# Dilated attention's last head pair: its small transfers on ScalarE's DMA queue, one token tile held back for it, four head-pair outputs split ahead of the last tile of values

## The chip, the cores and the metric

The kernel runs on one core of one Trainium2 chip. A time is the device time of one execution in microseconds (us). Before the change it is 2256.52 us, the median of three runs from 2256.39 to 2257.5.

A core has a matrix engine (TensorE, in the profile PE, with its weight loads as PEld), a vector engine (VectorE, DVE), an activation engine (ScalarE, ACT), GpSimd (POOL) and SyncE (SP), which here does nothing but issue DMA transfers. The engines run side by side, each works through its own instructions in order, and they wait for one another through semaphores. Matrix products land in eight banks of PSUM.

## The reference, cut to what matters

Two decoder layers on 512 tokens of width 1024. Each layer is feed-forward, token mixer, feed-forward; layer 0 mixes with latent attention, layer 1 with dilated attention. The change lies at the end of layer 1's mixer. Per head (16 of them, 64 wide) and per dilation group (three), that is:

```python
s = einsum(q, k) * E ** -0.5 + bias          # windows of dilation 1, 4, 16
lse = logsumexp(s); p = exp(s - lse)
o_g = einsum(p, v)                           # g = 0, 1, 2
alpha = softmax([lse_0, lse_1, lse_2])       # over the three groups, per token and head
o = sum_g alpha_g * o_g
y = o.reshape(S, 1024) @ w_o
x = x + gate * rmsnorm(y)                    # then the next sub-layer's norm, shift and scale
```

The kernel computes the sum over groups as one softmax: one common minimum (of negated scores) over the three groups, the exponentials of all groups against it, one common sum, one division at the end.

## The kernel before, in words

All weight products run in three passes: an operand is split into a high part (`hi`, rounded to fp32r) and a low part (`lo = x - hi`), and `mm3` (L147 to L149) adds hi·hi, hi·lo and lo·hi. `weights` (L132, L134) loads a weight of 512 KB through SP, casts `whi` on ScalarE and subtracts `wlo` on VectorE in two halves. `put_o` (L708, L709) does the same with one head pair's output.

**Pairs and slots.** Heads are taken in eight pairs, 0 to 7. `rest` of class `Dil` is a written-out order for TensorE, ScalarE and VectorE; SP's and GpSimd's order, and everything behind `rest`, is left to the scheduler. For pairs 0 to 6 each slot n puts a piece of the pair's attention beside the projection of the next pair. The last pair has no further projections to stand beside. What it gets are one tile of values (`tile(7, 2)`) and the first half of the output product, `part(0)` to `part(7)`: four token tiles by two halves of the width, each summed over output weights 0 to 3 (`early = 4`), with its result copied by VectorE at L465.

**What a pair does.** `scores` gives q·k per block and, on VectorE (L1144), the negated scores with their minimum per row, tile `dm`. Groups 0 and 2 keep their rows in other orders than group 1, so the minima take a way through DRAM to meet:

- `tops_out`: `natural` writes `dm` of group 0 in one transfer (L1164) and of group 2 in four (L1166) to `m0`; one read brings both back in group 1's order (x<-m, L1175).
- `tops`: two VectorE minima (L1182, L1183), a write to `t0` (t<-y, L1184), then read back in group 0's order (L1185) and group 2's (four transfers, L1187).
- `exps`: ScalarE's exponentials with their sums `dz` (L1203). Step 2 is group 1, step 3 is group 2, steps 0 and 1 are group 0.
- `norm`: the sums go the same way as the minima did (z<-dz, `natural` again, and x<-z, L1219).
- `norm_out`: two additions and a reciprocal on VectorE (L1227 to L1229), a write (d<-w, L1230), and two reads of 128 KB that spread it over 64 rows each (s<-d, L1233).
- `turn` and `weigh`: transposes of the exponentials and their products with the values; `finish` (L1306) multiplies the result by the reciprocals.

All these transfers are issued by SP, between its loads of weights and of the parked residual (x<-park, L518; w_gu belongs to the next feed-forward network).

**The end.** Behind `rest`, `transition` runs `tail(i)` for token tiles i = 0 to 3: output weights 4 to 7, added to the parts at L463 and squared at L314. Weight 7 belongs to the last pair. So for the first `waiting` token tiles the sums over weights 4 to 6 are opened at once in PSUM banks, ahead of the last pair's result, and only weight 7's products follow behind it. Each tile then passes the norm's square root on GpSimd (L321, L322), the residual (L503) and the next norm (L337, L338); 13 three-pass products behind tile 1 its transposes (L527) and the modulation (L305 to L311) follow, and then the heads, the first three units of the next feed-forward network for tokens 0 to 255.

**Around the change**, the order in `rest` is: slot (7,0), splits of outputs 0 to 2, `tile(7, 2)`, slot (7,1) (it has the scores of groups 1 and 2), the division for pair 6, the split of output 3, `part(0)`, splits of 4 and 5, `part(1)`, `tops`, group 1's exponentials, pair 6's finish and split, parts 2 to 5, the other exponentials, `norm`, and the rest of the pair beside parts 6 and 7.

Of the kernel before, what the change touches and what calls it, by code (L numbers as in the profile page):

```python
# [7 lines left out]
F32 = mybir.dt.float32  # L8
# [6 lines left out]
P = 128  # L15
SEQ = 512
# [22 lines left out]
def f(ap):  # L39
    return ap.bitcast(F32)  # L40
# [495 lines left out]
class Ffn:  # L536
# [92 lines left out]
    def rest(self):  # L629
        t = self.t  # L630
        last = len(GROUPS) - 1
        for q, (at, n) in enumerate(GROUPS):
            if q == last - 1:
                t.gates(self)
            for ft in range(max(at, START if t.first is self else HEAD), at + n):
                self.head(ft, 0, SEQ)
                t.pump(3 if t.first is self else 2)
            for i in range(TT if q < last else 0):
                self.down(q, i)
# [74 lines left out]
class Mla(Mixer):  # L714
# [5 lines left out]
    waiting = 1  # L720
# [37 lines left out]
    def norm(self, us, at, lo, hi):  # L758
        t, nc = self.t, self.t.nc
        n = hi - lo  # L760

        def total():
            r = t.root(t.sums([self.sq[u, lo] for u in us], n), n, P * len(us))
            t.after(5, lambda: apply(r))

        def apply(r):
            rb = t.spread(r, n)
            for j, u in enumerate(us):
                if lo == 0:
                    self.latn[u] = [t.s(F32R) for _ in range(2)]  # L770
                hh, hl = [x[:, lo:hi] for x in self.latn[u]]
                v = t.t("u", UB)[:, :n]
                nc.vector.scalar_tensor_tensor(
                    v, self.lat[u][:, lo:hi], t.glat[:, at + j : at + j + 1], rb, ALU.mult, ALU.mult
                )
                nc.scalar.activation(hh, v, AF.Copy)
                nc.vector.tensor_tensor(hl, v, f(hh), ALU.subtract)

        t.after(4, total)
# [185 lines left out]
class Dil(Mixer):  # L965
# [2 lines left out]
    late = False  # L968
    busy = True
    early = 4  # L970
    waiting = 2
    w_o = "dil_o"
    BLOCKS = (
        (0, ((0, 384, 128, 0), (1, 256, 256, 0))),
# [183 lines left out]
    def biases(self, p):  # L1158
        self.bias[p] = [self.bias_of(2 * p + e) for e in range(2)]

    def natural(self, dram, src):

        nc = self.t.nc
        nc.sync.dma_start(dram[0].rearrange("(j p) v -> p j v", p=P), src[:, 0])  # L1164
        for a in range(4):
            nc.sync.dma_start(  # L1166
                dram[1].rearrange("(l a j) v -> a l j v", a=4, j=4)[a], src[32 * a : 32 * a + 32, 2]
            )

    def tops_out(self, pair):  # L1170
        t = self.t
        m0 = t.dram.tile([2, SEQ, 2], F32, tag="m0", name="m0", bufs=2)
        self.natural(m0, pair["m"])
        x = pair["x"] = t.tmp.tile([P, 2, 4, 2], F32, tag="x4", name="x4", bufs=2)
        t.nc.sync.dma_start(x, m0.rearrange("g (p r) v -> p g r v", r=4))  # L1175

    def tops(self, pair):
        t, nc = self.t, self.t.nc
        m, x = pair["m"], pair["x"]
        t0 = t.dram.tile([SEQ, 2], F32, tag="t0", name="t0", bufs=2)  # L1180
        top = t.tmp.tile([P, 3, 4, 2], F32, tag="y4", name="y4", bufs=2)
        nc.vector.tensor_tensor(top[:, 1], x[:, 0], x[:, 1], ALU.min)  # L1182
        nc.vector.tensor_tensor(top[:, 1], top[:, 1], m[:, 1], ALU.min)  # L1183
        nc.sync.dma_start(t0.rearrange("(p r) v -> p r v", r=4), top[:, 1])  # L1184
        nc.sync.dma_start(top[:, 0], t0.rearrange("(j p) v -> p j v", p=P))  # L1185
        for a in range(4):
            nc.sync.dma_start(  # L1187
                top[32 * a : 32 * a + 32, 2], t0.rearrange("(l a j) v -> a l j v", a=4, j=4)[a]
            )
        pair["top"] = top  # L1190

    def exps(self, p, us):
        nc = self.t.nc
# [16 lines left out]
                    )  # L1210
                    at += n

    def norm(self, pair):
        t, nc = self.t, self.t.nc
        z = pair["z"]
        z0 = t.dram.tile([2, SEQ, 2], F32, tag="z0", name="z0", bufs=2)
        self.natural(z0, z)
        x = pair["x"] = t.tmp.tile([P, 2, 4, 2], F32, tag="x4", name="x4", bufs=2)
        nc.sync.dma_start(x, z0.rearrange("g (p r) v -> p g r v", r=4))  # L1219

    def norm_out(self, pair):
        t, nc = self.t, self.t.nc
        x, z = pair["x"], pair["z"]
        d0 = t.dram.tile([2, SEQ], F32, tag="d0", name="d0", bufs=2)
        d = t.tmp.tile([P, 2, 4], F32, tag="w4", name="w4", bufs=2)
        dr = d.rearrange("p e r -> p r e")
        nc.vector.tensor_tensor(dr, x[:, 0], x[:, 1], ALU.add)  # L1227
        nc.vector.tensor_tensor(dr, dr, z[:, 1], ALU.add)
        nc.vector.reciprocal(d, d)  # L1229
        nc.sync.dma_start(d0.rearrange("e (p r) -> p e r", r=4), d)  # L1230
        r = pair["r"] = t.s()
        for e in range(2):
            nc.sync.dma_start(r[64 * e : 64 * e + 64], d0[e : e + 1].broadcast_to([64, SEQ]))  # L1233


    TURNS = (
# [155 lines left out]

    def beside(self, p, n):
        if n == 1 and p:
            self.norm_out(self.pairs[p - 1])
        elif n == 2 and p:
            self.finish(p - 1)
        elif n == 3:
            self.tops(self.pairs[p])
            self.exps(p, (2,))  # L1400
        elif n == 4:
            self.exps(p, (0, 1))

    def behind(self, p, n):
        if n == 5:
            self.exps(p, (3,))
            self.norm(self.pairs[p])

    def rest(self):
        t = self.t  # L1410
        t.gates(self)
        self.of = []
        self.bias = {}
        self.coming, self.loaded, self.at = self.loads(), 0, 0
        with t.tc.manual_schedule(engines={PE, ACT, DVE}):
            self.ahead(SLOTS - 2)
            self.biases(0)
            for p in range(7):
                values = [(p, g, j) for g in range(3) for j in range(4) if p in self.BLOCKS_V]
                for n, at in enumerate([(p + 1, u) for u in self.ORDER] + values):  # L1420
                    self.slot(p, n)
                    self.ahead(self.at + min(SLOTS - 1 + max(n - 6, 0) % 4, SLOTS))
                    self.beside(p, n)
                    if n < 6:
                        self.tile(*at, 0, SEQ)
                    else:
                        self.value_tile(*at)
                    self.behind(p, n)
                    if n < 6 or n % 4 == 1:
                        self.at += 1 if n < 6 else 4  # L1430
            self.slot(7, 0)
            self.ahead(self.at + SLOTS - 1)
            for x in self.of[:3]:
                self.put_o(x)
            self.tile(7, 2, 0, SEQ)
            self.slot(7, 1)
            self.ahead(self.at + SLOTS + 1)
            self.norm_out(self.pairs[6])
            self.put_o(self.of[3])
            t.new_y()  # L1440
            self.part(0)
            self.later()
            for x in self.of[4:]:
                self.put_o(x)
            self.part(1)
            self.tops(self.pairs[7])
            self.exps(7, (2,))
            self.finish(6)
            self.put_o(self.of[-1])
            for n in range(2, 6):  # L1450
                self.part(n)
            self.exps(7, (3, 0, 1))
            self.norm(self.pairs[7])
            self.turn(7, 2)
            self.part(6)
            self.turn(7, 3)
            self.part(7)
            self.turn(7, 0)
            self.weigh(7, 2, 2, 1)
            self.turn(7, 1)  # L1460
            for n in (3, 0):
                self.weigh(7, n, 2, 1)
            self.norm_out(self.pairs[7])
            self.weigh(7, 1, 2, 1)
        for i in range(TT):
            t.unpark(i)
        self.finish(7)
        self.put_o(self.of[-1])
# [119 lines left out]
```

## Time and profile before

| | |
|---|---|
| median of three runs | 2256.52 us (2256.39 to 2257.5) |
| the profiled execution | 2258.68 us, its span 2256.5 us |
| TensorE busy | 2217.8 us, 98% |
| VectorE busy | 1183.6 us, 52% |
| ScalarE busy | 848.3 us, 38% |
| mean granted TensorE clock | 0.996 of full |
| last pair's result multiplied (L1306) | at 1860.06 us of the span |

The span runs from the first instruction to the last. An engine's row gives busy time; the idle time just before an instruction is put down to what released it. In the chain of waits each row is a start, a length and what ran; `DMA d<-w` is the time from the issue of that transfer to its landing. `SPq` is SP issuing a transfer. A small busy share far from 1 says nothing by itself: what counts is which wait ends last at a place.

### The profile page before, as it was taken

Reading aid. Unit: us, or ns where it says so; the run is one execution under the profiler, and the core shown is the slowest. Engines: PE = TensorE matmul, PEld = TensorE weight load, DVE = VectorE, ACT = ScalarE, POOL = GpSimd, SP = SyncE. Lnnn points to the kernel's source line nnn. Section 1 sums busy time; section 2 is a strip of 40 time slices with the busy share of each in tenths; the row PEclk is TensorE's granted clock in tenths of the full one; section 3 lists DMA queues with packets and bytes.
Section 4 is the critical chain, followed back from the end, with each engine's and each line's share of the span. In section 5 each row is a group of like instructions: output and inputs, shape, how many; then the busy total and the mean of one; then the engine's idle time right before and its main releaser. Section 6 shows DMA issues by size and latency. Waiting matters only on the chain. (4 is left out here: it accounts for less than half of the span.)

```text
span 2256.5 us, 30151 instructions
## 1 busy us (share of the span) xinstructions
PE 2217.8 (98%) x11354; PEld 1868.9 (83%) x11354; DVE 1183.6 (52%) x2691; ACT 848.3 (38%) x1730; POOL 106.3 (5%) x143
## 2 busy tenths in 40 slices
PE   7999999999999999999999999999999998999998
PEld 5888888877898888898888889988899878888887
DVE  7666575677665356474464463234424466333344
ACT  4422234577633132352221353434342545322232
POOL 1000001210110000020000010000000002000000
PEclk9999999999999999999999999999999999999999
DMA  8575762311255365334653533334343442233231
GB/s 309 158 245 186 195 219 69 110 52 57 66 167 181 110 187 181 127 121 136 175 179 119 159 117 111 101 103 93 72 114 110 89 129 66 83 120 101 79 112 38
DMA packets 124056, 290.33 MB, mean 129 GB/s; under 512 B 44786, under 2 KB 49157, under 8 KB 123910
## 3 DMA queue, kind: packets, MB, share of 16 engines
q1 hardware_dynamic: 123910, 288.41, 41.6%
q8 instruction: 89, 1.46, 0.3%
q14 instruction: 57, 0.47, 0.1%
HBM read 281.76 MB, written 4.49 MB: 127 GB/s over the span
## 5 line engine op out<-in xcount | busy, mean ns | idle before, releaser
L134 DVE TENSOR_TENSOR wlo<-raw,whi 128x512 fp32r<-128x512 f32 (+1 forms) x714 | 467.4, 692 | 593.8 <-ACT whi L132 592.6
L147 PE MATMUL mm<-s,whi 128*128 128x512 f32 (+1 forms) x1932 | 722.1, 374 | 2.4 <-ACT whi L132 2.4
L149 PE MATMUL mm<-s,wlo 128*128 128x512 f32 (+1 forms) x1932 | 719.2, 372 | 0.0
L148 PE MATMUL mm<-s,whi 128*128 128x512 f32 (+1 forms) x1932 | 719.0, 372 | 0.0
L132 ACT ACTIVATE whi<-raw 128x1024 fp32r<-128x1024 f32 (+1 forms) x357 | 368.8, 1048 | 785.2 <-PE mm L148 531.6
L147 PEld LDWEIGHTS mm<-s,whi 128*128 128x128 f32 x1932 | 364.3, 189 | 69.3 <-issue 3.5
L149 PEld LDWEIGHTS mm<-s,wlo 128*128 128x128 f32 x1932 | 364.6, 189 | 63.5
L148 PEld LDWEIGHTS mm<-s,whi 128*128 128x128 f32 x1932 | 364.6, 189 | 61.7
L147 PE MATMUL mm<-whi,s 128*128 128x512 f32 (+1 forms) x1040 | 407.1, 391 | 4.1 <-ACT s L708 4.1
L149 PE MATMUL mm<-whi,s 128*128 128x512 f32 (+1 forms) x1040 | 404.7, 389 | 1.2 <-DVE s L709 1.2
L148 PE MATMUL mm<-wlo,s 128*128 128x512 f32 (+1 forms) x1040 | 405.2, 390 | 0.0
L147 PEld LDWEIGHTS mm<-whi,s 128*128 128x128 f32 x1040 | 211.2, 203 | 39.7 <-ACT s L708 4.5
L149 PEld LDWEIGHTS mm<-whi,s 128*128 128x128 f32 x1040 | 211.3, 203 | 36.1 <-DVE s L709 1.6
L148 PEld LDWEIGHTS mm<-wlo,s 128*128 128x128 f32 x1040 | 211.3, 203 | 34.0 <-issue 0.3
L169 DVE CUSTOM_DVE_ANT_0 raw<-raw,cs 128x1024 f32<-128x1024 f32 x130 | 159.4, 1232 | 124.4 <-DMA raw<-w_mod 123.9
L463 DVE TENSOR_TENSOR s<-mm,s 128x512 f32<-128x512 f32 x112 | 76.8, 690 | 121.1 <-PE mm L149 121.1
L322 POOL TENSOR_TENSOR mv<-mv,mhalf 128x1 f32<-128x1 f32 x48 | 36.2, 756 | 1493.5 <-DVE mv L321 1491.0
L1092 ACT ACTIVATE s<-mm 128x128 f32<-128x128 f32 (+3 forms) x109 | 33.1, 358 | 163.6 <-PE mm L149 159.7
L586 ACT ACTIVATE s<-gg 128x512 fp32r<-128x512 f32 (+1 forms) x97 | 57.4, 592 | 47.1 <-DVE gg L585 47.1
L585 DVE TENSOR_TENSOR gg<-silu,mm 128x512 f32<-128x512 f32 (+1 forms) x95 | 59.9, 630 | 12.0 <-ACT silu L583 12.0
L1203 ACT ACTIVATE u<-u,y 128x128 f32<-128x128 f32 x128 | 49.6, 397 | 23.8 <-issue 13.1
L583 ACT ACTIVATE silu<-mm 128x512 f32<-128x512 f32 (+1 forms) x95 | 51.4, 541 | 18.3 <-PE mm L149 18.2
(185 smaller groups left out, 1682.7 us busy)
## 6 DMA issues: line engine op xcount, KB each, us to landing
raw<-w_gu SPq DMA_DIRECT2D x168, 512.0 KB, 4.2
raw<-w_mod SPq DMA_DIRECT2D x130, 512.0 KB, 4.6
raw<-w_down SPq DMA_DIRECT2D x88, 512.0 KB, 4.3
raw<-dil_in SPq DMA_DIRECT2D x47, 512.0 KB, 4.1
raw<-dil_v SPq DMA_DIRECT2D x20, 512.0 KB, 3.7
s<-w_mod SPq DMA_DIRECT2D x28, 256.0 KB, 5.7
raw<-w_gu SPq DMA_DIRECT2D x16, 256.0 KB, 3.7
raw<-mla_o SPq DMA_DIRECT2D x8, 512.0 KB, 3.9
```

Of the source, the lines that this page charges most:

```text
L132: self.nc.scalar.activation(hi, raw, AF.Copy)
L134: self.nc.vector.tensor_tensor(lo[:, r], raw[:, r], f(hi[:, r]), ALU.subtract)
L147: mm(out, w[0], m[0], start=first, stop=False)
L148: mm(out, w[0], m[1], start=False, stop=False)
L149: mm(out, w[1], m[0], start=False, stop=last)
L169: nc.vector.tensor_tensor_reduce(raw, raw, self.cs, 1.0, 0.0, ALU.mult, ALU.add, accum_out=t[:, 0:1])
L322: nc.gpsimd.tensor_tensor(v[:, 1:2], v[:, 0:1], self.mhalf[:, 0:1], ALU.pow)
L463: nc.vector.tensor_tensor(y, b, y, ALU.add)
L583: nc.scalar.activation(s, banks[0], AF.Silu)
L585: nc.vector.tensor_tensor(v, s, banks[1], ALU.mult)
L586: nc.scalar.activation(ghi, v, AF.Copy)
L1203: nc.scalar.activation(c, c, AF.Exp, bias=pair["top"][:, g, i, one], scale=-1.0, accum_out=pair["z"][:, g, i, one],)
```

## The change

- Outputs 0 to 3, not 0 to 2, are split ahead of `tile(7, 2)`; the split of output 3 behind slot (7,1) goes.
- For the last pair, the transfers of `tops`, `norm` and `norm_out` are issued by ScalarE in place of SP. Its first transfers (`tops_out`) and those of all other pairs stay on SP.
- `tops` is cut in two: the write, and the reading back (`tops_back`), which for the last pair stands behind group 1's exponentials.
- `natural` is cut into `near` (group 0) and `far` (group 2). For the last pair `norm_far` sends group 2's sums as soon as that group's exponentials are done, ahead of group 0's.
- One token tile, not two, is opened ahead of the last pair's result (`waiting = 1`).

```diff
-    waiting = 2
+    waiting = 1
...
-    def natural(self, dram, src):
-        nc.sync.dma_start(dram[0].rearrange("(j p) v -> p j v", p=P), src[:, 0])
+    def near(self, dram, src, queue):
+        queue.dma_start(dram[0].rearrange("(j p) v -> p j v", p=P), src[:, 0])
+    def far(self, dram, src, queue):
         for a in range(4):
-            nc.sync.dma_start(
+            queue.dma_start(
                 dram[1].rearrange("(l a j) v -> a l j v", a=4, j=4)[a], src[32 * a : 32 * a + 32, 2]
             )
...
-        nc.sync.dma_start(t0.rearrange("(p r) v -> p r v", r=4), top[:, 1])
-        nc.sync.dma_start(top[:, 0], t0.rearrange("(j p) v -> p j v", p=P))
+        queue.dma_start(t0.rearrange("(p r) v -> p r v", r=4), top[:, 1])
+
+    def tops_back(self, pair, queue):
+        t0, top = pair["t0"], pair["top"]
+        queue.dma_start(top[:, 0], t0.rearrange("(j p) v -> p j v", p=P))
         for a in range(4):
-            nc.sync.dma_start(
+            queue.dma_start(
                 top[32 * a : 32 * a + 32, 2], t0.rearrange("(l a j) v -> a l j v", a=4, j=4)[a]
             )
...
+    def norm_far(self, pair, queue):
+        t = self.t
+        z0 = pair["z0"] = t.dram.tile([2, SEQ, 2], F32, tag="z0", name="z0", bufs=2)
+        self.far(z0, pair["z"], queue)
+
+    def norm(self, pair, queue):
+        t, z0 = self.t, pair["z0"]
+        self.near(z0, pair["z"], queue)
         x = pair["x"] = t.tmp.tile([P, 2, 4, 2], F32, tag="x4", name="x4", bufs=2)
-        nc.sync.dma_start(x, z0.rearrange("g (p r) v -> p g r v", r=4))
+        queue.dma_start(x, z0.rearrange("g (p r) v -> p g r v", r=4))
...
-            for x in self.of[:3]:
+            for x in self.of[:4]:
                 self.put_o(x)
             self.tile(7, 2, 0, SEQ)
             self.slot(7, 1)
             self.ahead(self.at + SLOTS + 1)
-            self.norm_out(self.pairs[6])
-            self.put_o(self.of[3])
+            self.norm_out(self.pairs[6], t.nc.sync)
             t.new_y()
             self.part(0)
...
-            self.tops(self.pairs[7])
+            last, queue = self.pairs[7], t.nc.scalar
+            self.tops(last, queue)
             self.exps(7, (2,))
+            self.tops_back(last, queue)
             self.finish(6)
             self.put_o(self.of[-1])
             for n in range(2, 6):
                 self.part(n)
-            self.exps(7, (3, 0, 1))
-            self.norm(self.pairs[7])
+            self.exps(7, (3,))
+            self.norm_far(last, queue)
+            self.exps(7, (0, 1))
+            self.norm(last, queue)
...
-            self.norm_out(self.pairs[7])
+            self.norm_out(last, queue)
             self.weigh(7, 1, 2, 1)
```

More of the change, by code (lines that the diff above doesn't have):

```diff
@@ L1159, in biases @@
         self.bias[p] = [self.bias_of(2 * p + e) for e in range(2)]
-    def natural(self, dram, src):
-        nc = self.t.nc
-        nc.sync.dma_start(dram[0].rearrange("(j p) v -> p j v", p=P), src[:, 0])
+    def near(self, dram, src, queue):
+        queue.dma_start(dram[0].rearrange("(j p) v -> p j v", p=P), src[:, 0])
+    def far(self, dram, src, queue):
         for a in range(4):
-            nc.sync.dma_start(
+            queue.dma_start(
                 dram[1].rearrange("(l a j) v -> a l j v", a=4, j=4)[a], src[32 * a : 32 * a + 32, 2]
@@ L1172, in tops_out, with tops @@
         m0 = t.dram.tile([2, SEQ, 2], F32, tag="m0", name="m0", bufs=2)
-        self.natural(m0, pair["m"])
+        self.near(m0, pair["m"], t.nc.sync)
+        self.far(m0, pair["m"], t.nc.sync)
         x = pair["x"] = t.tmp.tile([P, 2, 4, 2], F32, tag="x4", name="x4", bufs=2)
         t.nc.sync.dma_start(x, m0.rearrange("g (p r) v -> p g r v", r=4))
-    def tops(self, pair):
+    def tops(self, pair, queue):
         t, nc = self.t, self.t.nc
         m, x = pair["m"], pair["x"]
-        t0 = t.dram.tile([SEQ, 2], F32, tag="t0", name="t0", bufs=2)
-        top = t.tmp.tile([P, 3, 4, 2], F32, tag="y4", name="y4", bufs=2)
+        t0 = pair["t0"] = t.dram.tile([SEQ, 2], F32, tag="t0", name="t0", bufs=2)
+        top = pair["top"] = t.tmp.tile([P, 3, 4, 2], F32, tag="y4", name="y4", bufs=2)
         nc.vector.tensor_tensor(top[:, 1], x[:, 0], x[:, 1], ALU.min)
         nc.vector.tensor_tensor(top[:, 1], top[:, 1], m[:, 1], ALU.min)
-        nc.sync.dma_start(t0.rearrange("(p r) v -> p r v", r=4), top[:, 1])
-        nc.sync.dma_start(top[:, 0], t0.rearrange("(j p) v -> p j v", p=P))
+        queue.dma_start(t0.rearrange("(p r) v -> p r v", r=4), top[:, 1])
+    def tops_back(self, pair, queue):
+        t0, top = pair["t0"], pair["top"]
+        queue.dma_start(top[:, 0], t0.rearrange("(j p) v -> p j v", p=P))
         for a in range(4):
-            nc.sync.dma_start(
+            queue.dma_start(
                 top[32 * a : 32 * a + 32, 2], t0.rearrange("(l a j) v -> a l j v", a=4, j=4)[a]
             )
-        pair["top"] = top
     def exps(self, p, us):
@@ L1211, in exps, with norm_out @@
                     at += n
[L1213 to L1217, printed above, removed]
+    def norm_far(self, pair, queue):
[5 more added lines that the diff above has]
+        self.near(z0, pair["z"], queue)
         x = pair["x"] = t.tmp.tile([P, 2, 4, 2], F32, tag="x4", name="x4", bufs=2)
-        nc.sync.dma_start(x, z0.rearrange("g (p r) v -> p g r v", r=4))
-    def norm_out(self, pair):
+        queue.dma_start(x, z0.rearrange("g (p r) v -> p g r v", r=4))
+    def norm_out(self, pair, queue):
         t, nc = self.t, self.t.nc
@@ L1229, in norm_out @@
         nc.vector.reciprocal(d, d)
-        nc.sync.dma_start(d0.rearrange("e (p r) -> p e r", r=4), d)
+        queue.dma_start(d0.rearrange("e (p r) -> p e r", r=4), d)
         r = pair["r"] = t.s()
         for e in range(2):
-            nc.sync.dma_start(r[64 * e : 64 * e + 64], d0[e : e + 1].broadcast_to([64, SEQ]))
+            queue.dma_start(r[64 * e : 64 * e + 64], d0[e : e + 1].broadcast_to([64, SEQ]))
     TURNS = (
@@ L1394, in beside @@
         if n == 1 and p:
-            self.norm_out(self.pairs[p - 1])
+            self.norm_out(self.pairs[p - 1], self.t.nc.sync)
         elif n == 2 and p:
@@ L1398, in beside @@
         elif n == 3:
-            self.tops(self.pairs[p])
+            self.tops(self.pairs[p], self.t.nc.sync)
+            self.tops_back(self.pairs[p], self.t.nc.sync)
             self.exps(p, (2,))
@@ L1406, in behind @@
             self.exps(p, (3,))
-            self.norm(self.pairs[p])
+            self.norm_far(self.pairs[p], self.t.nc.sync)
+            self.norm(self.pairs[p], self.t.nc.sync)
     def rest(self):
```

## The prediction

> **What bounds the kernel now.** I began with the busy shares on the page: TensorE leaves little open over the whole program, so the change can win only where TensorE stands still.
>
> ```profile
> PE 2217.8 (98%) x11354; PEld 1868.9 (83%) x11354; DVE 1183.6 (52%) x2691; ACT 848.3 (38%) x1730; POOL 106.3 (5%) x143
> ```
>
> Next the waits of TensorE between 1820 and 1895 us, the end of the dilated stage and the change to the last feed-forward network (sum, times, longest):
>
> ```profile
> PE mm L147 <- ACT s L708: 4.1, 1, 4.1
> PE mm L147 <- ACT s L310: 3.1, 1, 3.1
> PE aux L527 <- ACT s L337: 1.7, 1, 1.7
> PE mm L148 <- POOL s L307: 1.2, 1, 1.2
> PE mm L149 <- DVE s L709: 1.2, 1, 1.2
> PE mm L148 <- DVE s L311: 0.5, 1, 0.5
> ```
>
> These six make 11.8 us. Put in order of time: 1.2 on the split of the fourth output (L709), 4.1 on the split of the eighth, which is the last pair's result (L708), and 6.5 in the transition that follows (the L337, L310, L311 and L307 waits). 11.8 us plus a slow-clock stretch is all the time that this change can reach. The stretches around them (length, busy PE, PEld, DVE, ACT, POOL with instructions, granted clock, DMA share, GB/s):
>
> ```profile
> 1842.00:1846.00 4.00, 3.86 (x35) 2.99 (x34) 3.24 (x6) 3.21 (x5) 0.00 (x0) 1.00 0.06 1
> 1848.00:1857.50 9.50, 9.38 (x48) 7.20 (x44) 4.01 (x9) 1.06 (x1) 0.00 (x0) 1.00 0.94 299
> 1861.50:1865.30 3.80, 3.79 (x10) 2.97 (x11) 2.58 (x4) 1.62 (x4) 0.00 (x0) 0.55 0.00 0
> 1865.30:1877.50 12.20, 12.18 (x56) 9.74 (x54) 11.78 (x24) 7.92 (x24) 2.25 (x4) 1.00 0.15 44
> 1877.50:1891.00 13.50, 7.01 (x50) 6.05 (x51) 12.65 (x25) 12.00 (x26) 5.67 (x7) 1.00 0.48 155
> ```
>
> From 1865.3 to 1891 VectorE is busy 24.4 of 25.7 us while TensorE idles 6.5: after the last pair has arrived, VectorE sets the pace. Before that, nobody does; a chain of small transfers runs there, which the chain of waits shows (start, length, what):
>
> ```profile
> 1827.18 4.68 DMA t<-y
> ...
> 1833.31 0.42 SPq L1187
> 1833.77 1.56 DMA y<-t
> 1835.43 3.20 ACT u L1203 x16
> 1838.63 3.44 ACT sq L1203 x15
> 1842.39 4.09 DMA z<-dz
> 1846.50 1.73 DMA x<-z
> 1848.43 0.59 DVE wlo L134
> 1849.18 0.44 issue
> 1849.84 5.03 DMA d<-w
> 1854.89 0.45 SPq L1233
> 1855.39 4.55 DMA s<-d
> 1860.06 0.70 DVE s L1306
> ```
>
> I call 1860.06 the arrival A. Of the 33 us before it, transfers take 21.6. The d<-w and s<-d steps run while the DMA engines are 0.94 busy; z<-dz runs while they are idle (0.06), so its 4.09 us are its own.
>
> **The change, part by part.** *The fourth output's split* (hi and lo) moves ahead of the last tile of values and so ahead of the scores of slot (7,1). The 1.2 us wait goes, but TensorE then only comes 1.2 us sooner to the wait for A: alone it is worth nothing. VectorE pays one L709 earlier and pushes the minima of those scores back:
>
> ```profile
> 1821.74 0.64 DVE L709 TENSOR_TENSOR s<-s 128x512 fp32r<-128x512 f32 x1
> ```
>
> The minimum over the groups sits behind the second output part's copy, which comes up to 1.2 sooner, and behind a transfer that starts up to 0.6 later. Bounds -1.2 to +0.6; I take -0.3, the middle, because no row says which of the two came last.
>
> *The tops on ScalarE's queue.* ScalarE now issues the write t<-y, runs eight exponentials, and only then issues the read-backs. Eight such exponentials with their reads are the row of 16 in the chain, 3.2 us; with an issue of 0.42 before it (a price taken from SP's L1187, as no row shows an issue on ScalarE) the read-back goes out 3.6 us behind the minima instead of 4.7: -1.1, and no more however fast the write lands, since ScalarE works in order. If the write keeps its 4.68, it is 0. Queued behind the read-backs on ScalarE are the seventh output's split and the exponentials of group 2, which wait for the same data anyway.
>
> *norm_far on ScalarE.* Before, SP sent these four beside the exponentials; now they stand between the two sets of them:
>
> ```profile
> 1838.65 1.89 SPq L1166 DMA_DIRECT2D z<-dz  x4
> ```
>
> So +1.7 (four times 0.42) on the path; if ScalarE issues nearly free, +0.2, and if each takes 0.96, the longest issue of SP's L1164, +3.8. I take +1.7, the same kind of instruction.
>
> ```profile
> L1164 SPq DMA_DIRECT2D m<-dm x1: 956/956/956, 1810.4 to 1810.4; - x1
> ```
>
> *norm and norm_out.* The transfers' times to landing over all pairs (median, last number):
>
> ```profile
> s<-tv SPq DMA_DIRECT2D x16, 128.0 KB, 3.4
> ...
> x<-z SPq DMA_DIRECT2D x8, 8.0 KB, 3.9
> d<-w SPq DMA_DIRECT2D x8, 4.0 KB, 3.1
> ```
>
> z<-dz stays at 4.09 (idle engines; 0 to +0.7, as loads may now run beside it). x<-z took 1.73 with quiet engines; SP no longer blocks on it, so the loads that stand behind it go out some 2 us sooner and meet it:
>
> ```profile
> 1846.98 0.41 SPq L124 DMA_DIRECT2D raw<-w_gu  x1
> 1847.48 0.86 SPq L518 DMA_DIRECT2D x<-park  x2
> ```
>
> Up to +2.2 (3.9 less 1.73); I take +0.4, because in another queue it doesn't stand behind them. d<-w was issued at 1849.84, behind these three loads of 512 KB in the same queue; in another I take the median 3.1: -1.9 (0 if it stays, -3.3 at x<-z's 1.73). s<-d: the nearest row of its size is s<-tv with 3.4: -1.15 (0, or -2.8). Between them the two wlo subtractions that part the three small VectorE steps of norm_out stay; if they go, -1.2.
>
> A wait is new on ScalarE: it stands on z<-dz before it can issue x<-z. What may queue behind are three weight casts:
>
> ```profile
> 1842.27 2.94 ACT L132 ACTIVATE whi<-raw 128x1024 fp32r<-128x1024 f32 x3
> ```
>
> ```profile
> 1843.35 1.29 DVE L134 TENSOR_TENSOR wlo<-raw,whi 128x512 fp32r<-128x512 f32 x2 [0.76 <-ACT whi L132]
> ```
>
> The first of them should be the seventh output weight's, which the open products need only behind two others. If all go out 4.5 us later, they end at 1849.7, well before A, so I put it at 0, hidden by TensorE's wait for A; should their subtractions (two per weight, 1.3 us) fall behind A, 3.9 us of VectorE follow.
>
> *One token tile waits.* At the full clock a product takes this much of the chain:
>
> ```profile
> 1865.42 0.23 PE mm L147
> ```
>
> 18 products (one tile, three weights, two halves, three passes), 4.1 us, move from ahead of A to behind it. TensorE gets to the wait 1.2 + 4.1 sooner and idles longer; at both ends it has the same work.
>
> **Sum.** Arrival: -0.3 - 1.1 + 1.7 + 0 + 0.4 - 1.9 - 1.15 = -2.35, A' = 1857.7. Behind the arrival, tile 1's last product has 30 products ahead instead of 12, 4.1 us more. The heads that need tile 1 started only at the second row here (the first is the last of tile 1's transposes):
>
> ```profile
> 1879.14 1.53 PE L527 MATMUL aux<-ident,s 128*128 128x128 f32 x12 [1.66 <-ACT s L337]
> 1883.79 0.50 PE L147 MATMUL mm<-s 128*128 128x256 f32 x2 [3.12 <-ACT s L310]
> ```
>
> That is A + 23.7, some 18 us behind tile 1's last product, most of it queued on a VectorE that was handed two tiles at once. Now tiles come 24 products (5.5 us) apart, near the 6.1 us that a quarter of VectorE's 24.4 makes, so I expect the 4.1 to be taken out of that queue. TensorE's own work runs from A' + 1.45 (L1306, L708 and the gaps): nine products at the slow clock in 3.8 us (the stretch with clock 0.55 has ten), 69 at 0.227 (15.7), 16 transposes (2.1, as 12 take 1.53), to A' + 23.1. I take the heads at A' + 23.3, 0.4 sooner. Bounds: 2.4 sooner (the moved products fill 4.1 of the 6.5 idle, and no wait is left) to 4.1 later (they fill none). In all -2.75. With every term at its best end it would be -11.8, at its worst +11.4; they won't meet. The profiled execution took 2258.68 (span 2256.5 and 2.2 around it), 2.2 more than the median of the runs, 2256.52; the same step from that median gives **2253.8**.
>
> **The rivals.** *The engines are the limit, not the queue*: d<-w and s<-d keep 5.03 and 4.55. For it: share 0.94 at 299 GB/s; against: x<-z needs 1.73 when nothing stands ahead. Arrival +0.7, heads 0.4 sooner: +0.3, 2256.8. Chance 0.2. That the change doesn't do what it says, the transfers ending up in one queue after all, gives the same time and is in this chance.
> The Trainium skill, page "DMA: Bandwidth & Descriptors", section "Issuing engines are not separate DMA queues", is on this rival's side: DMAs of several engines run on the same 16 DMA engines, and issuing from another saves only sequencer time. The same page's "Queues, rings and completion order" has each engine take packets from its queues in turn, which would spare a small transfer the loads ahead of it and is on the forecast's. The trace of before has SP's hardware queue alone and can't decide.
> *The queue clears wholly*: d<-w and s<-d both take x<-z's 1.73, 3.05 us less than I took: -5.8, 2250.7. For it: the two are small; against: s<-tv, the same 128 KB, has a median of 3.4. Chance 0.2.
> *Slower: the chain behind tile 1 keeps its 18 us.* Place: VectorE and ScalarE between tile 1's last product and the heads. Price +4.1 on A', less 2.35: +1.75, 2258.3; with the first rival's arrival +4.8, 2261.3. It decides once more than 2.35 of the 4.1 stay. For it: ScalarE too is 12.0 of 13.5 us busy there; against: VectorE's queue is shorter when tiles come apart. Chance 0.15.
>
> **How the numbers follow.** The forecast has 0.45. 0.2% is 4.5 us, about what a measurement of this kernel tells from no change. Faster by more: the second rival's 0.2 and a fourth of the forecast's, its lower tail (d<-w below 3.1 or heads sooner): 0.32. Slower by more: half of the slower rival (0.08) and the case of dear issues on ScalarE (0.03): 0.11. Within: the rest, 0.57. The range goes from 2248.5 (the second rival, and heads as early as their bound) to 2260 (between the two forms of the slower rival); the forecast's own is 2251 to 2256.5.
>
> **What would show it.** Right: t<-y to read-back 3.6 us; the four z<-dz issues on ScalarE 1.7; d<-w near 3.1 and s<-d near 3.4; the wait on L708 some 7 us (TensorE there 5.3 sooner, the result 2.35); less than 4 us of waits in the transition. Wrong: s<-d still near 4.5 (first rival); heads more than 25 us behind the arrival (third); a wait of TensorE ahead of the open products (weight casts blocked on ScalarE).

## The result and the profile after

After the change the kernel takes 2264.87 us (median, 2262.99 to 2265.88); runs of the kernel before, taken beside it on the same chip, have a median of 2256.45. The ratio is 1.0038, 95% interval [1.0025, 1.0051]: slower, by 8.4 us. I had forecast 2253.8 in a range of 2248.5 to 2260. The profiled execution took 2265.5 us against 2258.68 before, 6.8 more (spans 2263.4 and 2256.5), so the two traces can be set side by side; they show 6.8 of the 8.4 us, since the kernel before was profiled in an execution 2.2 above its median, and the kernel after in one 0.6 above.

Besides SP's queue, q1, the page of the kernel after has a second one (packets, MB, share):

```profile
q10 hardware_dynamic: 2288, 0.30, 0.1%
```

So the transfers did go into a queue of their own, ScalarE's. The waits of TensorE in the kernel after, 1820 to 1902 us (sum, times, longest):

```profile
PE mm L147 <- ACT s L708: 11.7, 1, 11.7
PE mm L147 <- ACT s L310: 3.1, 1, 3.1
PE aux L527 <- ACT s L337: 1.7, 1, 1.7
```

The wait on the fourth output's split (L709, 1.2) is gone, the transition's waits are what they were, and the wait for the last pair has grown from 4.1 to 11.7. The chain of waits of the kernel after shows why (start, length, what):

```profile
1822.72 6.60 DMA x<-m
...
1829.74 0.36 ACTq L1187
...
1831.50 0.22 ACTq L1191
1831.72 0.17 ACT u L1208 x2
...
1833.26 1.69 DMA y<-t
...
1840.05 3.83 ACT sq L1208 x16
1843.92 5.00 DMA z<-dz
1848.94 7.66 DMA x<-z
1856.63 0.18 DVE w L1235
...
1857.28 2.47 DMA d<-w
...
1860.35 5.12 DMA s<-d
1865.60 0.70 DVE s L1314
```

The arrival (L1306 before, L1314 now) went from 1860.06 to 1865.60, 5.54 later. Step by step, from the starts in the two chains: the write of the tops goes out 2.56 later; write and read-back win that back and 0.37 more; four issues between the exponentials cost 1.90; z<-dz 0.91; **x<-z 5.93**; VectorE's three small steps win 0.93, d<-w 2.48; s<-d costs 0.58. Without x<-z the arrival would stand where it stood.

Behind the arrival comes one more loss. A stretch of the kernel after (length, busy PE, PEld, DVE, ACT, POOL with instructions, granted clock, DMA share, GB/s):

```profile
1867.00:1873.40 6.40, 6.34 (x15) 4.98 (x16) 4.67 (x9) 2.38 (x7) 0.65 (x1) 0.52 0.00 1
```

It follows the long wait: the clock stays near half for 6.4 us, where it was 3.8 us at 0.55 before. Its length doesn't grow with the wait, though: in the runs below it was 3.3 us at 0.51 behind a wait of 8.7 (e8) and 6.2 us at 0.51 behind one of 4.1 (e6). So what this stretch costs can't be put down to the wait being longer. The first product of the heads in the kernel after:

```profile
1890.61 0.80 PE L147 MATMUL mm<-s 128*128 128x256 f32 x2 [3.12 <-ACT s L310]
```

The heads start at 1890.61 in place of 1883.79, 6.8 later: 5.54 from the arrival and 1.3 from here.

### The profile page after: what moved, and what is told of

It is laid out like the page before. It is cut to its first block, busy times and chain, and to the rows that moved or that the text cites. A ratio compares the mean times of both kernels' runs of the same rounds, so it can differ in the third digit from the quotient of the medians.

```text
span 2263.4 us, 30143 instructions
## 1 busy us (share of the span) xinstructions
PE 2220.8 (98%) x11354; PEld 1870.1 (83%) x11354; DVE 1181.9 (52%) x2691; ACT 848.6 (37%) x1730; POOL 106.5 (5%) x143
## 3 DMA queue, kind: packets, MB, share of 16 engines
q1 hardware_dynamic: 121622, 288.11, 41.7%
HBM read 281.76 MB, written 4.49 MB: 126 GB/s over the span
## 4 chain that ended last, share of the span: by engine, by line
PE 90%; DVE 3%; ACT 2%; issue 2%; DMA 1%; POOL 1%; ACTq 0%; SPq 0%; POOLq 0%; DVEq 0%
PE mm L147 28%; PE mm L148 28%; PE mm L149 28%; PE mm L879 1%; PE mm L1127 1%; PE aux L1294 1%; PE aux L1261 1%; PE aux L928 1%; POOL mv L322 1%; PE aux L907 1%; PE aux L527 0%; DVE x L503 0%; DVE wlo L134 0%; DMA x<-z 0%; ACT whi L132 0%
## 5 line engine op out<-in xcount | busy, mean ns | idle before, releaser
L147 PE MATMUL mm<-whi,s 128*128 128x512 f32 (+1 forms) x1040 | 407.8, 392 | 12.3 <-ACT s L708 11.7
```

The lines of the kernel that those rows point to most:

```text
L147: mm(out, w[0], m[0], start=first, stop=False)
```

## The experiments

Each stage of a trace is read from the start of the four `m<-dm` issues (1818.91 before, 1818.24 after), because the profiled executions come to that point up to 3.5 us apart. Behind that point the last pair arrives after 41.15 us before and 47.36 after. *Theory L*: what slows a small transfer is the loads of 512 KB that run beside it, whichever queue it stands in. *Rival Q*: ScalarE's queue is slow in itself. *Rival S*: the split, not the queue, did it. Ratios are against runs of the kernel before on the same chip, whose medians were 2255.6 to 2256.89 us.

**e1_split_only.** The kernel before with only the fourth output's split moved.

```diff
-            for x in self.of[:3]:
+            for x in self.of[:4]:
...
-            self.put_o(self.of[3])
```

> The kernel before with one edit: output 3's split moves ahead of the last tile of values; all transfers stay on SP, two token tiles wait. Theory L (loads that SP sends earlier run into the small transfers): the wait of TensorE on L709 (1.2 us) goes; x<-m, which the changed kernel's SP issues behind two 256 KB loads, lands at about 1829.3 as in the changed kernel (6.6 us) and not by 1826.8, but the write t<-y then goes out 2.5 us later into quieter engines and lands in 2 to 3 us, not 4.7, so the arrival (start of L1306 or its like) is 1860 to 1861.5 and the median 2256 to 2258. Rival S (the split is the cause): arrival 2.5 us or more later, 2259 to 2262. The prediction's own step (worth nothing alone): 2256.

2258.33 us, ratio 1.0009 [1.0000, 1.0019]. From its chain:

```profile
1822.82 6.09 DMA x<-m
1829.33 1.80 DMA t<-y
...
1845.49 3.51 DMA x<-z
1850.61 4.69 DMA d<-w
```

With the split ahead, SP's order puts two loads of 256 KB in front of x<-m, which then takes 6.09 us; the loads that used to stand in front of t<-y are past by then, and t<-y takes 1.80 in place of 4.68. The two cancel, and the arrival is at 41.7. So the 2.56 us in the chain after, and its fast tops, are the split's; they are worth nothing together, and by its median rival S has a quarter of the loss, by its interval between none and half of it.

**e2_queue_only.** The change without the split, and with `waiting` at 2 again.

```diff
-    waiting = 1
+    waiting = 2
...
-            for x in self.of[:4]:
+            for x in self.of[:3]:
...
             self.norm_out(self.pairs[6], t.nc.sync)
+            self.put_o(self.of[3])
```

> The changed kernel without the moved split (output 3 split where it was before; two token tiles, which gives the same program as one). ScalarE issues the last pair's transfers. Theory L: x<-m lands by 1826.8 again; t<-y on ScalarE then runs amid the loads, and if a queue of its own doesn't spare it, takes 4 us or more, if it does, about 2; x<-z again runs into the two parked tiles and two weight loads and takes 6 to 8 us; arrival 1863 to 1866, median 2261 to 2265. Rival S (the split is the cause of the loss): median 2254 to 2257.

2263.62 us, ratio 1.0034 [1.0021, 1.0046]: nearly the whole loss. Its chain:

```profile
1824.39 6.37 DMA t<-y
...
1847.88 8.38 DMA x<-z
1856.93 2.27 DMA d<-w
```

Without the split t<-y meets the loads in ScalarE's queue and takes 6.37, longer than behind them in SP's (4.68). In e3 and e4, which have the same order there, it takes 5.20 and 5.17. x<-z is slow again, amid five loads of 512 KB as in the change: two parked tiles and three weights, the first issued 4.1 us before it and the last 1.4 behind it.

**e3_sums_on_sp.** e2 with the sums' way (`norm_far`, `norm`) back on SP.

```diff
-            self.norm_far(last, queue)
+            self.norm_far(last, t.nc.sync)
...
-            self.norm(last, queue)
+            self.norm(last, t.nc.sync)
```

> As the run with the queue only, but the sums' transfers (four z<-dz of group 2, z<-dz of group 0, x<-z) go back to SP; tops and norm_out stay on ScalarE. In SP's order the late loads then stand behind x<-z. Theory L: x<-z takes 1.7 to 2 us, the four z<-dz no longer part the exponentials (1.8 us less), z<-dz near 4.1; then d<-w and s<-d run amid the loads: 2.5 to 3.1 and 3.5 if a queue of its own spares them, 5 or more each if not. Arrival 1853 to 1857 in the first case (median 2250 to 2254), 1857 to 1861 in the second. Rival Q (ScalarE's queue is slow in itself): x<-z fast here too, but t<-y, d<-w and s<-d each 1 us or more above their times on SP wherever they run.

2261.69 us, ratio 1.0023 [1.0013, 1.0032].

```profile
1845.65 1.70 DMA x<-z
1848.97 7.17 DMA d<-w
```

x<-z is back at 1.70, and the loads that SP now sends behind it meet d<-w, which is still on ScalarE: 7.17 us, against 5.03 behind the loads in SP's own queue. The slow transfer moved with the loads.

**e4_hold_parked.** e2 with the last two parked tiles held until x<-z has landed; in SP's order the third weight then stands behind them. A VectorE copy of one column writes to each tile first.

```diff
         for i in range(TT):
-            t.unpark(i)
+            if i < 2:
+                t.unpark(i)
+                continue
+            t.x[i] = t.wide()
+            t.nc.vector.tensor_copy(t.x[i][:, 0:1], last["x"][:, 0, 0, 0:1])
+            t.nc.sync.dma_start(t.x[i], t.parked[i])
```

> As the run with the queue only, but the reads of the last two parked tiles wait for x<-z (a copy of one column by VectorE, two copies, about 0.2 us, stands between); x<-z stays on ScalarE. Two weight loads still come ahead of it. Theory L: with half of the loads out of its way x<-z falls from about 7.7 to 3 to 5 us and the arrival comes 2 to 4 us sooner than with the queue only. Rival Q (ScalarE's queue is slow in itself): x<-z stays at 7 or more.

2262.2 us, ratio 1.0023 [1.0013, 1.0032].

```profile
1847.69 4.43 DMA x<-z
1852.80 4.73 DMA d<-w
```

Two loads beside x<-z in place of five: 4.43 us in place of 8.38. The parked tiles now meet d<-w instead, 4.73 in place of 2.27.

**e5_loads_behind_xz** and **e6_loads_behind_sd_act.** e2 with all loads held: three one-column VectorE steps read the buffers of the last three output weights, so that these come free only behind the reciprocal (e5) or behind s<-d (e6). The last two parked tiles are held as in e4, in e6 on the tile of s<-d. For this the loads and casts of output weights 6 and 7 are listed behind `norm`. The diff is e6's; in e5 the step is a copy of `raw`. An added line, which keeps a list of the weight buffers, makes the line numbers one higher from here on, but for e8 and e11.

```diff
             self.norm(last, queue)
+            for j in (6, 7):
+                self.out_weights(j)
...
+            held = t.tmp.tile([P, 8], F32, tag='held', name='held', bufs=1)
+            for q, raw in enumerate(t.raws[-3:]):
+                t.nc.vector.tensor_tensor(held[:, q : q + 1], raw[:, 0:1], self.pairs[7]['r'][:, 0:1], ALU.add)
```

> All of e2_queue_only's transfers on ScalarE, but no load of 512 KB can go out before the last pair's reciprocal: the buffers of the last three output weights are kept until then by one-column copies on VectorE, and the last two parked tiles wait for x<-z in the same way. Theory L (what slows a small transfer is the loads that run beside it, whichever queue it is in): x<-z on ScalarE's queue falls from 8.38 to 1.7 to 2.2 us, the 1.73 that it takes in SP's queue; d<-w, which now meets the released loads, takes 5 to 7.2 as in e3_sums_on_sp. Arrival behind the start of m<-dm 48.9 - 6.4 + 3 = 45 to 47. Rival Q (ScalarE's queue, or its issues beside running activations, are slow in themselves): x<-z stays above 4 us.

> As e5_loads_behind_xz, but the loads are held until s<-d has landed, so the whole chain on ScalarE's queue runs without them. Theory L: x<-z 1.7 to 2.2, d<-w 2.3 to 2.5, s<-d about 3.0; arrival 48.9 - 6.4 - 2.1 = 40.4 us behind the start of m<-dm, against 48.9 in e2_queue_only and 41.15 in the kernel before; time 2263.6 - 8.5 = 2255 if nothing behind it comes late. Rival (the loads are missed later): arrival as said, but TensorE's heads wait for gate and up weights or for their casts, and the time stays above 2258.

e5: 2269.45 us, ratio 1.0057 [1.0042, 1.0071], arrival at 48.8. e6: 2261.1, 1.0022 [1.0013, 1.0031], arrival at 44.5. Both arrivals came later than expected, because of the listing: the two casts stand behind ScalarE's wait for z<-dz, and VectorE's order takes their subtractions and the copies behind them ahead of `norm_out`. The chain of e6:

```profile
1845.49 0.38 ACTq L1228
1845.92 1.06 ACT whi L133
1847.00 2.50 DVE wlo L135 x4
...
1856.12 1.56 DMA d<-w
...
1858.23 3.32 DMA s<-d
```

x<-z is issued at 1845.49 (1845.18 in e5) and is in no chain, so its landing can't be read here; but the DMA queues have all its 272 packets moved within 1.5 us of the issue in both runs. And d<-w on ScalarE's queue takes 1.56 us with no loads about (e6) and 4.52 with them (e5). Rival Q has fallen for d<-w, and by the packets for x<-z.

e5's time is higher than its arrival explains: from the first product of the heads to the end of the span it needs 375.8 us, e2 372.8. Where these 3 us went stays open.

**e7_loads_behind_sd_sp** and **e11_casts_pinned.** The same hold, and the same listing, in the kernel before, all transfers on SP (e7); and the listing without the hold (e11).

> The kernel before, every transfer on SP as it was, and only the loads moved: in SP's order all loads of 512 KB stand behind the last pair's s<-d. Theory L: x<-z 1.7, d<-w 2.3 to 2.5 in place of 5.03, s<-d 3.0 in place of 4.55: arrival 4.2 us sooner, 37 us behind the start of m<-dm; this is what the change wanted, without a second queue. Time 2252.3 if nothing behind comes late (before 2256.4). Rival (the loads are missed later): about 2.5 MB that went out from 1847 to 1857 go out some 10 us later, their casts fall into the stretch where VectorE is nearly full, and the heads start no sooner: 2256 to 2258.

> The kernel before with the loads and casts of output weights 6 and 7 listed behind norm, as in e7_loads_behind_sd_sp, and no load held: what of e7's 4.5 us belongs to this step. Theory L: nothing of it; d<-w 4.5 to 5 and s<-d 4 to 5 as before, norm_out later by the subtractions ahead of it (in e7 it began at 1850.0, 1.7 later than before): 2256 to 2259. Rival (the casts' place is what helped): 2252 to 2253.

e7: 2252.33 us, ratio 0.998 [0.9971, 0.9988], the first that is faster than the kernel before; arrival at 38.6. e11: 2258.07, 1.001 [1.0001, 1.0019], arrival at 42.4. e11's chain still has d<-w amid loads:

```profile
1852.13 4.28 DMA d<-w
```

So the listing costs, and the hold is what won.

**e8_one_tile_open.** The kernel before, with one open token tile made real: tiles 1 to 3 take output weight 7 as their first product.

```diff
+                js = list(range(self.early, KT))
+                js = js if self.late else js[-1:] + js[:-1]
+                self.products(b, i, d, js, (js[:1], js[-1:]))
...
-    waiting = 2
+    waiting = 1
```

> The kernel before, with the change's waiting = 1 made to bite: token tiles 1 to 3 take output weight 7, the last pair's, as their first product, so that none of their products can run ahead of the last pair's result. 18 products of tile 1 then really stand behind the arrival. My prediction's step: the heads start 0.4 us sooner to 0 later at an unchanged arrival (bounds -2.4 to +4.1), time 2256 to 2256.5; the wait on L708 grows from 4.1 by 4.1 to about 8. The slower rival (the chain behind tile 1 keeps its 18 us): heads 4.1 later, 2260.5.

2257.38 us, ratio 1.0005 [0.9996, 1.0015]. A wait of TensorE, and its first product of the heads, in e8 (L714 is L708 there):

```profile
PE mm L147 <- ACT s L714: 8.7, 1, 8.7
```

```profile
1882.20 0.38 PE L147 MATMUL mm<-s 128*128 128x256 f32 x1 [1.75 <-ACT s L310]
```

The wait grows by 4.6, and the heads start 24.4 us behind the arrival (1857.79) in place of 23.7. Of the 4.1 us of moved products about 0.7 stay; the time can't be told from before.

**e9_change_and_hold** and **e10_hold_alone.** The hold without the listing: `out_weights(6)` and `(7)` and the three one-column steps stand behind the last pair's finish, so that the scheduler places the casts where it did before; the last two parked tiles are held on the tile of s<-d. e9 is the change as made with this hold, e10 the kernel before with it.

```diff
         self.finish(7)
         self.put_o(self.of[-1])
+        for j in (6, 7):
+            self.out_weights(j)
+        held = t.tmp.tile([P, 8], F32, tag="held", name="held", bufs=1)
+        for q, raw in enumerate(t.raws[-3:]):
+            t.nc.vector.tensor_tensor(held[:, q : q + 1], raw[:, 0:1], self.pairs[7]["r"][:, 0:1], ALU.add)
```

> The change as made, all of it, and the loads of 512 KB held behind s<-d: the buffers of the last three output weights and of the last two parked tiles are kept by one-column VectorE steps that read the tile of s<-d; the weight casts are left where the scheduler puts them (in e6_loads_behind_sd_act I had pinned two of them, and they pushed norm_out to 1855.5). Theory L: on ScalarE's queue x<-z 1.7 to 2.2 us in place of 7.66, d<-w 1.56 as in e6 and e7, s<-d 3.0 to 3.3; two casts still stand behind ScalarE's wait for z<-dz and their subtractions ahead of norm_out, some 2 us. Arrival 37 to 39 us behind the start of m<-dm (after 47.36, before 41.15), time 2252 to 2255. Rival Q (ScalarE's queue is slow in itself for x<-z): x<-z above 4, arrival above 40, time above 2256.

> The kernel before with the loads alone held behind s<-d in SP's own queue, casts left to the scheduler: e7_loads_behind_sd_sp without the pinned casts. Theory L: x<-z 1.7, d<-w 1.5, s<-d 3.0, t<-y 3.2 as in e7 (no load of 512 KB ahead of it): arrival 41.15 - 3.5 - 1.5 - 1.4 = 34.7 us behind the start of m<-dm. TensorE's wait there was 1.3 us in e7 at 38.6 and is gone, so only that 1.3 is left to win against e7: 2251. Rival (the loads, 10 us later, are missed by the heads): 2253 to 2256.

e9: 2252.65 us, ratio 0.9986 [0.9977, 0.9995]. **e10: 2250.19 us, ratio 0.9973 [0.9962, 0.9983]**, faster than both kernels of this case. The chain of e9:

```profile
1848.65 1.92 DMA x<-z
...
1851.24 1.55 DMA d<-w
...
1853.34 3.02 DMA s<-d
```

SP's issues in e10 (start, length, line, transfer):

```profile
1843.16 0.38 SPq L1220 DMA_DIRECT2D x<-z  x1
1847.06 0.36 SPq L1231 DMA_DIRECT2D d<-w  x1
1848.73 1.09 SPq L1234 DMA_DIRECT2D s<-d  x2
1852.76 0.81 SPq L1472 DMA_DIRECT2D x<-park  x2
1853.62 2.91 SPq L124 DMA_DIRECT2D raw<-w_gu  x4
```

On ScalarE's queue without loads x<-z takes 1.92 us, d<-w 1.55 and s<-d 3.02; on SP's without loads d<-w lands 1.67 after its issue (1847.06 to the next step's 1848.73). Without loads the queue makes next to no difference (x<-z 1.92 against 1.70 to 1.81 ahead of the loads on SP's, d<-w 1.55 against 1.67); amid them x<-z took 4.43 to 8.38 us and d<-w 4.28 to 7.17: rival Q is refuted, theory L holds. Amid loads ScalarE's queue was no shelter but rather the worse place: t<-y took 5.17 to 6.37 us there (e2, e3, e4), on SP's 4.23 to 4.82 (before, e8, e11). The arrivals, 37.0 (e9) and 35.0 (e10), are in or near what was expected. TensorE's two longest waits there in e10 (1820 to 1902 us):

```profile
PE aux L528 <- ACT s L338: 2.3, 1, 2.3
PE mm L148 <- ACT s L311: 2.2, 1, 2.2
```

The wait for the last pair is gone, and so is the slow stretch behind it. The gate and up weights, sent from 1853 rather than 1847, hold up the heads no more than before (2.2 against 3.1 on L310, here L311). One of them now lies on the chain behind the arrival, though (raw<-w_gu, 6.78 us from 1855.15), so they could hardly go out later at no cost. Against e10 the change's own parts cost 2.5 us even with the loads away.

## Why the prediction was wrong

**x<-z: the step that failed.** I took +0.4 with a bound of +2.2, "because in another queue it doesn't stand behind them". It measured 7.66, +5.93. That is 5.5 of the 7.9 us by which the arrival missed my sum. The prediction saw that SP would no longer block and that the loads would go out sooner; it took the second queue for a shelter. These are the issues of the kernel after (SP, then ScalarE):

```profile
1844.55 0.81 SPq L518 DMA_DIRECT2D x<-park  x2
1847.15 13.37 SPq L124 DMA_DIRECT2D raw<-w_gu  x4
```

```profile
1848.94 0.38 ACTq L1227 DMA_DIRECT2D x<-z  x1
```

Before, SP itself waited for z<-dz, so two parked tiles and a weight stood behind x<-z; SP's waiting was the shelter, and the change took it away. Now the two tiles and two weights go out ahead of x<-z and a third weight 0.6 us behind it; only the fourth waits, until 1860.19. The DMA queues in two stretches of x<-z in the kernel after, 1848.93 to 1852.25 and 1852.25 to 1856.60 (packets, MB, share):

```profile
q1 hardware_dynamic: 328, 1.20, 100.2%
```

```profile
q1 hardware_dynamic: 340, 1.21, 69.5%
q10 hardware_dynamic: 272, 0.01, 3.5%
```

For 3.3 us after its issue not one of x<-z's packets moves, while 1.20 MB of loads do; then its 272 packets pass among 340 of the loads in 4.3 us. In e9 the same transfer is done in 1.92 us, and its first packet moves 1.0 us behind the issue:

```profile
q10 hardware_dynamic: 272, 0.01, 7.7%
```

The second part, two queues sharing the engines, is what the Trainium skill, page "DMA: Bandwidth & Descriptors", section "Queues, rings and completion order", would lead one to expect, by which each DMA engine takes packets from its queues in turn. How many pieces of a small transfer pass in a turn isn't fixed by the runs: 272 beside 340 of the loads here, 164 beside 108 in the densest microsecond of e2. The first part, the late first packet, that rule does not give. It comes again in e2 (x<-z, 3.7 us or more), in e3 (d<-w, 3.0 or more) and with two loads in e4 (x<-z, 2.0 or more), and no run here says where it comes from.

**One token tile waits: nothing moved.** I let 18 products go behind the arrival. With `waiting = 1` the scheduler still puts tile 1's products ahead of the wait. TensorE's products for the open sums ahead of the wait, before (1848.99 to 1861.45), after (two stretches, the first ahead of `weigh`) and in e8:

```profile
1848.99:1861.45 12.46, 8.39 (x36) 6.60 (x36) 0.00 (x0) 0.00 (x0) 1.00 0.82 258
```

```profile
1841.60:1843.84 2.24, 1.89 (x6) 0.98 (x6) 0.67 (x1) 0.00 (x0) 1.00 0.00 0
...
1848.25:1867.04 18.79, 7.07 (x30) 5.52 (x30) 0.00 (x0) 0.00 (x0) 0.80 0.51 177
```

```profile
1846.30:1859.24 12.94, 4.23 (x18) 3.16 (x18) 0.00 (x0) 0.00 (x0) 0.86 0.81 252
```

36, 6 + 30, and 18 only where e8 forces it. That the change doesn't do what it says was a rival of mine for the queue; it was true of this part, and I had not asked it there. The step's other half, that VectorE's queue absorbs the products, was nearly right: 0.7 later in e8 where I had 0.4 sooner. The slower rival, with 4.1 that stay, is refuted by e8; the result was slower for another reason. The heads did start 25.0 us behind the arrival in the kernel after, which I had named as that rival's sign, but with the same 36 products ahead of the wait as before it can't be its mechanism.

**The split: -0.3** (bounds -1.2 to +0.6). The minima came 2.56 later. I weighed VectorE's few tenths and not SP's order, in which two loads moved ahead of x<-m.

**The tops: -1.1 "and no more however fast the write lands".** They gained 2.93. The bound rested on ScalarE issuing the read-back only behind its eight exponentials; the chain after has the issue of L1191 at 1831.50 between exponentials. By the timeline it starts at 1831.35, 1.6 us behind the write's issue where I had 3.6. The write itself was fast because the split had let the loads pass; in e2 it took 6.37.

**norm_far: +1.7.** 1.90: right, and at the price that I took from SP's issues (the four take 1.73). **z<-dz: 0 to +0.7.** 0.91. Two parked tiles now went out beside it, but that they are the cause isn't shown: with no load about the same step took from 3.72 (e6) to 4.49 (e9), 4.09 before. **The wlo subtractions: 0, or -1.2 if they go.** They went, 0.93: the weight casts ran ahead of ScalarE's wait (from 1843.79), and their subtractions were over when x<-z landed.

**d<-w: -1.9, s<-d: -1.15.** d<-w gained 2.56, but only since x<-z was so late that the loads were over (2.27 in e2 too); s<-d lost 0.57. I had priced s<-d by s<-tv's 3.4, though the same list has s<-d itself over all pairs at 4.1. Where d<-w did meet loads in ScalarE's queue it took 4.52 to 7.17 (e5, e4, e3), SP's 4.28 to 5.03 (e11, e8, e1, before). The rival "the engines are the limit, not the queue" was the right one in kind, as the second queue spared a small transfer nothing; its time, 2256.8, was too low since it too left x<-z alone. What the rival "the queue clears wholly" counted on, d<-w at 1.73, comes without loads (1.55 and 1.56); s<-d then takes 3.0 to 3.3.

**The wait on L708: "some 7".** 11.7: the arrival 5.54 later, and TensorE there 2.1 sooner, its last product issued at 1854.93 in place of 1857.00. I had 5.3 sooner, 4.1 of it for the products that did not move.

## What to carry to other kernels

When a small transfer is moved to another queue, list what the old queue's owner was kept from issuing while it waited: those loads go out sooner and meet the transfer, and a second queue does not shelter it from them. What frees a chain of small transfers is that the large loads stand behind it; a buffer that comes free a little later, by a one-column read, is enough to put them there, and here it beat the second queue by 12 us of the arrival (47.36 to 35.0) and 2264.87 to 2250.19 us in time. And a setting that a scheduler may override is looked up in the order of instructions before its effect is priced.

## What the runs showed of the hardware

- **Place against queue.** x<-z (8 KB): 1.70 to 1.81 us ahead of the loads in SP's queue (before, e3, e8), once 3.51 (e1); 7.66 and 8.38 on ScalarE's with five loads sent around it, 4.43 with two, 1.92 with none. In e1, 255 of its 272 packets were through by 1847.0, ahead of the loads' first; the others moved only among the loads, from 1847.5 on.
- **The first packet comes late.** 3.3 us after its issue amid loads, for a transfer whose first packet moves after 1.0 us without them (e9, and SP's queue in e10) and that is wholly done in 1.92.
- **ScalarE issues transfers between its activations**: in the chain after, the issue of the first read-back (L1191, 1831.50) stands between exponentials that the program lists ahead of it, and the last goes out at 1833.26, so an issue written behind activations need not wait for them all.
- **The slow clock follows the wait, and its length is not the wait's.** Behind TensorE's wait of 11.7 us the clock was 0.52 for 6.4 us, behind 8.7 us (e8) 0.51 for 3.3, behind 4.1 us 0.55 for 3.8 (before) and 0.51 for 6.2 (e6); in e9 a wait of 2.4 us was still followed by 0.53 for 3.4 us, in e7 one of 1.3 us by none (1.00 from 1857.80 on):

```profile
1858.00:1861.40 3.40, 3.36 (x8) 2.67 (x9) 2.12 (x4) 1.13 (x3) 0.00 (x0) 0.53 0.93 327
```

```profile
1857.80:1861.60 3.80, 3.78 (x17) 3.12 (x18) 3.62 (x6) 2.76 (x6) 0.00 (x0) 1.00 0.94 373
```

So a wait that goes from 4 us to nothing is worth its own length and, by an estimate from the kernel before, some 2 us more (ten products at 0.43 in place of 0.23); with the 15 products of the stretch in e6 it would be 3.
